# A mixer trunk on one core: another order of the second layer's chunks, and another cost for the first softmax step of a head pair

## The chip, the cores and the metric

The kernel runs on one core of a Trainium2 chip. A core has a matrix engine (TensorE; PE in the profile, its weight loads are PEld), a vector engine (VectorE, DVE), a scalar engine (ScalarE, ACT), GpSimd (POOL) and SyncE (SP), which issues the loads here. Each engine runs its own instructions in the order in which they stand in the program, and waits on semaphores for the others. The metric is the device time of one execution in microseconds (us); lower is better.

## The reference

Two layers work on 256 latent tokens with a prefix of 256 context tokens, width 2048. In each layer one projection of the normalised and modulated input feeds three groups of heads; a gate multiplies each, and one projection leads back:

```python
def _diff_attention(q, k, v, lam):
    ...
        s = jnp.einsum('bqhcd,bkhcd->bhcqk', qq, k).astype(jnp.float32) * scale
        p = jax.nn.softmax(s, axis=-1)
        a = p[:, :, 0] - lam * p[:, :, 1]
        return jnp.einsum('bhqk,bkhe->bqhe', a.astype(v.dtype), v)
```

This is attention with 8 heads, each with two softmaxes that are subtracted. Beside it run a pooling mixer over windows of 2 to 16 tokens, and a convolution module (a gated input, 31 taps, a layer norm, a pointwise product). Shift, scale and gate of each layer (adaLN) come from a vector c by a product with a large matrix, w_mod. Context tokens go through the first layer with the latents and serve the second only as keys and values.

## The kernel before

**Chunks and pieces.** The input projection has 26 chunks of 256 outputs. A chunk's name tells its group: q0 to q3, k0 to k3, v0 to v3 (queries, keys and values of head pairs 0 to 3), u0 and u1 (pool), a0, a1, b0, b1 (convolution), ga0 to ga3 (gates of attention), gp0, gp1 and gc0, gc1 (gates of pool and convolution). `project` computes one as four pieces, each of 24 TensorE products (float32 values are split in a high and a low part, and three of the four products are made). In the first layer there are 512 tokens and a piece has 512 columns (`FULL`); in the second only k and v are for all 512, the other chunks have 256 columns (`HALF`). `ORDER` and `ORDER_1` are the orders of the chunks in the first and the second layer, written by hand; the first layer's loop begins at k0, since b0, a0 and q0 are made while the adaLN sums come in.

**What runs beside the pieces.** After each piece `pump(us)` takes steps from four queues: the context rows of the next layer, `urgent` (attention, pool), `conv_work` and `mod_work`. Each step is a Python generator's, and yields a cost; the pump subtracts it and stops when nothing is left:

```python
    def pump(us):
        for q in (context_work, urgent, conv_work, mod_work):
            while q and us > 0:
                us -= step(q)
```

A pump has 3.4 after a full piece and 0.8 after a half one. `attention` is put in `urgent` when a v chunk is taken, and so runs beside the chunks that follow. `attend_front` makes the scores of one job (`sx`, latent queries; `sc`, context queries, first layer only) and their softmax: the maximum (`mxx`, VectorE, line 634), two exponentials (ScalarE, line 640), reciprocal and scaling (`rx`), and the combination `ex` (ScalarE line 648, VectorE line 649). `attend_back` transposes it on TensorE (`atx`, line 684), splits it in `ahx` (ScalarE) and `alx` (VectorE), and multiplies by the values (`ox`, lines 701 to 703). In names such as `ex0_6_0` the numbers are layer, head and query tile. Taking a q chunk drains `urgent`; taking u1 or v3 drains `conv_work`.

**The adaLN sums.** `mod_on_dve` loads w_mod in tiles of 512 KB (`mraw`, two buffers) and adds each up on VectorE (`macc`, lines 370 and 372), two instructions of it for a tile with two rows, one where only the latents need it. It is the last of the pump's queues. At the end of a unit of 16 tiles TensorE transposes the sums (`modt`). The last two units are put in the queue ahead of the second layer's v1 (`GATES_AT`).

**Order on the engines.** The scheduler of the tile framework places the instructions; each engine then runs them in that order. Weight splits (a cast on ScalarE, line 205, and a subtraction on VectorE, line 206; `in_q_h` and `in_q_l` for a q chunk) and the split of v are given a higher priority and so stand earlier than written. Score tiles and chunk sums share three PSUM buffers, transposes two.

Of the kernel before, what the change touches and what calls it, by code (L numbers as in the profile page):

```python
# [37 lines left out]
    "b0 a0 q0 k0 v0 u0 b1 a1 q1 k1 v1 q2 k2 v2 q3 k3 v3 u1 ga1 gc0 ga2 gp0 ga0 ga3 gp1 gc1"  # L38
).split()
ORDER_1 = (  # L40
    "b0 a0 q0 k0 v0 u0 b1 a1 q1 ga0 k1 v1 q2 k2 gc1 v2 q3 k3 v3 u1 ga1 ga3 gc0 ga2 gp1 gp0"
).split()
OFFSET = {"q": 0, "k": 1024, "v": 2048, "ga": 3072, "u": 4096, "gp": 4608, "a": 5120, "b": 5632, "gc": 6144}

# [7 lines left out]
MOD_TAGS = ("whi", "wlo", "mraw", "whi", "wlo", "mraw", "whi", "wlo")  # L52

FULL, HALF = 3.4, 0.8
FRONT_0 = 2.0
FRONT, BACK = 1.5, 0.7
WAIT_MOD = 4.0
WAIT_CONV = 3.0
# [11 lines left out]
def trunk(  # L70
# [30 lines left out]
    def tmp(name, dt=F32):  # L101
        return tp.tile([P, T], dt, tag="t", name=name)
# [4 lines left out]
    def bank(name):  # L107
        return tr.tile([P, T], F32, tag="tr", name=name)
# [33 lines left out]
    def rsqrt(v, n, name, a=None, y=None):  # L142

        if a is None:
            nc.gpsimd.tensor_tensor(out=v, in0=v, in1=half[:, 0:1].to_broadcast([P, n]), op=ALU.pow)
            return
        nc.vector.tensor_scalar(
            out=y.bitcast(I32), in0=v.bitcast(I32), scalar1=-0.5, scalar2=1597463007.0, op0=ALU.mult, op1=ALU.add
        )
        for step in range(3):  # L150
            nc.vector.tensor_mul(out=a, in0=y, in1=y)
            nc.vector.scalar_tensor_tensor(out=a, in0=a, scalar=-0.5, in1=v, op0=ALU.mult, op1=ALU.mult)
            nc.vector.scalar_tensor_tensor(out=v if step == 2 else y, in0=a, scalar=1.5, in1=y, op0=ALU.add, op1=ALU.mult)
# [469 lines left out]
    def take_v(L, p, ps):  # L623
        L.vh = at.tile([P, 4, WC], F32R, tag="vh", name=f"vh{L.l}_{p}")
        L.vl = at.tile([P, 4, WC], F32R, tag="vl", name=f"vl{L.l}_{p}")
        with tc.high_priority(offset=V_BY):
            split_act(L.vh, L.vl, ps.rearrange("p b (c n) -> p (b c) n", n=WC))
        urgent.append(attention(L, p))
# [33 lines left out]
    def attend_front(L, p, h, which, qt):  # L662

        name = f"{which}{L.l}_{2 * p + h}_{qt}"
        ps = mm.tile([P, 2, T], F32, tag="mm", name=f"s{name}")
        if which == "x":
            scores(L, ps, slice(0, T), h, slice(qt * P, (qt + 1) * P), slice(0, T))
        else:
            for q in range(2):
                scores(L, ps, slice(q * TL, (q + 1) * TL), h, slice(TL + q * P, TL + (q + 1) * P), slice(TL, T))  # L670
        return softmax(L, ps, T, 1, name) if which == "x" else softmax(L, ps, TL, 2, name)

    def attend_back(L, p, h, which, qt, a):
        head = 2 * p + h
        name = f"{which}{L.l}_{head}"
        if qt == 0:
            L.ah = at.tile([P, 4, TL], F32R, tag="ah", name=f"ah{name}")
            L.al = at.tile([P, 4, TL], F32R, tag="al", name=f"al{name}")
        ah, al = L.ah, L.al
        b = bank(f"at{name}_{qt}")  # L680
        if which == "x":
            k0, nk, ts, qs = 0, 4, slice(0, TL), slice(qt * P, (qt + 1) * P)
            for kt in range(4):
                nc.tensor.transpose(b[:, kt * P : (kt + 1) * P], a[:, kt * P : (kt + 1) * P], ident)
            split_act(ah[:, :, qs], al[:, :, qs], b.rearrange("p (k q) -> p k q", q=P))
            if qt == 0:
                return
        else:
            k0, nk, ts = 2, 2, slice(TL, T)
            bv = b.rearrange("p (k q) -> p k q", q=TL)  # L690
            for q in range(2):
                for kt in range(2):
                    nc.tensor.transpose(
                        bv[:, kt, q * P : (q + 1) * P], a[:, q * TL + kt * P : q * TL + (kt + 1) * P], ident
                    )
            split_act(ah[:, :2, :], al[:, :2, :], bv)
        o = bank(f"o{name}")
        hs = slice(h * P, (h + 1) * P)
        for i in range(nk):
            kt = k0 + i  # L700
            nc.tensor.matmul(o[:, :TL], lhsT=L.vh[:, kt, hs], rhs=ah[:, i, :], start=i == 0, stop=False)
            nc.tensor.matmul(o[:, :TL], lhsT=L.vh[:, kt, hs], rhs=al[:, i, :], start=False, stop=False)
            nc.tensor.matmul(o[:, :TL], lhsT=L.vl[:, kt, hs], rhs=ah[:, i, :], start=False, stop=i == nk - 1)
        nc.scalar.copy(out=L.y[head][:, ts], in_=o[:, :TL])
        if which == "x":
            L.osq[h] = tmp(f"osq{name}")
        nc.scalar.activation(L.osq[h][:, ts], o[:, :TL], AF.Square)

    def attention(L, p):
        l, n = L.l, L.n  # L710
        L.osq = [None, None]
        jobs = []
        for h in range(2):
            jobs += [(h, "x", 0), (h, "x", 1)] + ([(h, "c", 0)] if L.ctx else [])
        prev = None
        for j in jobs:
            a = attend_front(L, p, *j)
            yield FRONT if prev else FRONT_0
            if prev:
                attend_back(L, p, *prev)  # L720
                yield BACK
            prev = j + (a,)
        attend_back(L, p, *prev)
        yield BACK

        nh = n // 2
        b = bank(f"ssq{l}_{p}")[:, :nh]
        for h in range(2):
            for half in range(2):
                c = 32 * (2 * h + half)  # L730
                nc.tensor.matmul(
                    b[c : c + 32, :], lhsT=ones[:, 0:32], rhs=L.osq[h][:, half * nh : (half + 1) * nh],
                    start=True, stop=True, skip_group_check=True,
                )
        v = one.tile([P, TL], F32, tag=f"arv{p}", name=f"arv{l}_{p}")[:, :nh]
        nc.vector.tensor_scalar(out=v, in0=b, scalar1=1.0 / P, scalar2=EPS, op0=ALU.mult, op1=ALU.add)
        work = tmp(f"arw{l}_{p}")
        rsqrt(v, nh, f"ars{l}_{p}", work[:, :nh], work[:, TL : TL + nh])
        L.arstd[p] = v
        yield 4.0  # L740
# [488 lines left out]
```

## Time and profile before

| what | value |
|---|---|
| time, median of 3 runs | 1495.96 us (1493.52 to 1496.93) |
| the profiled execution's own time | 1502.84 us |
| its span in the trace | 1501.0 us |
| mean granted clock of TensorE | 0.992 of full speed |
| TensorE busy | 1452.5 us, 97% |
| VectorE busy | 1112.8 us, 74% |
| ScalarE busy | 650.2 us, 43% |
| bytes moved | 258.90 MB, 172 GB/s mean |

The times are of executions without a profile, the rows of one execution with it, whose own time stands in the second line. Starts in rows are us from the begin of its span. A busy share is of the span; the time that an engine stood still ahead of a row is the number in brackets at the row's end, with what ended the waiting behind the arrow.

### The profile page before, as it was taken

The numbers are of one execution on the slowest core, as the hardware profiler recorded it, in microseconds if no ns is written. First come the engines' busy times: TensorE is split into PE (matmuls) and PEld (weight loads), VectorE is DVE, ScalarE is ACT, GpSimd is POOL, SyncE is SP. The second block draws the span as 40 slices with busy tenths as digits, with TensorE's granted clock in tenths as the row PEclk, the third lists the DMA queues.
The fourth block names the chain that finished last, engine by engine and source line by source line (L and its number), as shares of the span: only waits on it lengthen the run. The fifth ranks groups of instructions, "written<-read, shape, count | busy, mean of one in ns | idle before, by whom it ended". The sixth has DMA issues, their size and how long they took to land.

```text
span 1501.0 us, 23277 instructions
## 1 busy us (share of the span) xinstructions
PE 1452.5 (97%) x9196; PEld 1241.8 (83%) x9196; DVE 1112.8 (74%) x1641; ACT 650.2 (43%) x1245; POOL 9.0 (1%) x46
## 2 busy tenths in 40 slices
PE   4999999999999999999999999999999999999997
PEld 3567977897797977888888889988989897999997
DVE  4446999997549865879898964998995567475655
ACT  4224363227546363332433242635545545464543
POOL 0000000000000000000000000000000000000000
PEclk9999999999999999999999999999999999999998
DMA  8995226432234613655667761436733264245553
GB/s 332 397 391 221 81 88 202 148 110 74 74 112 146 202 60 113 221 195 203 209 213 250 243 222 55 142 114 216 265 113 124 79 227 161 99 134 178 187 183 113
DMA packets 75855, 258.90 MB, mean 172 GB/s; under 512 B 8800, under 2 KB 11104, under 8 KB 75744
## 3 DMA queue, kind: packets, MB, share of 16 engines
q1 hardware_dynamic: 75456, 257.14, 49.2%
q8 instruction: 72, 1.18, 0.3%
q14 instruction: 39, 0.32, 0.1%
q10 hardware_dynamic: 288, 0.26, 0.1%
HBM read 255.27 MB, written 2.10 MB: 171 GB/s over the span
## 4 chain that ended last, share of the span: by engine, by line
PE 83%; DVE 7%; DMA 4%; issue 3%; ACT 2%; SPq 0%; POOL 0%; POOLq 0%; DVEq 0%; ACTq 0%
PE ps_o L236 16%; PE ps_k L236 12%; PE ps_ga L236 9%; PE ps_v L227 7%; PE ps_q L236 6%; PE ps_gc L236 5%; PE ps_gp L236 4%; PE ps_first L236 4%; PE ps_b L236 3%; PE ps_u L236 3%; PE ps_a L236 3%; DMA mraw<-in_w_mod 3%; PE modacc L336 2%; DVE s L479 2%; DVE macc L372 1%
## 5 line engine op out<-in xcount | busy, mean ns | idle before, releaser
L372 DVE SCALAR_TENSOR_TENSOR macc<-mraw,c_sb,macc 128x1024 f32<-128x1024 f32 x210 | 262.6, 1280 | 32.2 <-DMA mraw<-in_w_mod 31.5
L236 PE MATMUL ps_o<-yh,out_h 128*128 128x512 f32 (+1 forms) x448 | 151.7, 339 | 0.0
L236 PE MATMUL ps_o<-yl,out_h 128*128 128x512 f32 (+1 forms) x448 | 151.6, 338 | 0.0
L236 PE MATMUL ps_o<-yh,out_l 128*128 128x512 f32 (+1 forms) x448 | 151.6, 338 | 0.0
L227 PE MATMUL ps_v<-in_v_h,hh 128*128 128x256 f32 x512 | 145.2, 284 | 0.0
L227 PE MATMUL ps_v<-in_v_h,hl 128*128 128x256 f32 x512 | 144.8, 283 | 0.0
L227 PE MATMUL ps_v<-in_v_l,hh 128*128 128x256 f32 x512 | 144.3, 282 | 0.0
L479 DVE SCALAR_TENSOR_TENSOR s<-cu,vec,s 128x512 f32<-128x512 f32 (+1 forms) x240 | 136.5, 615 | 0.5
L205 ACT CAST out_h<-out_r 128x1024 fp32r<-128x1024 f32 x56 | 58.8, 1050 | 111.5 <-PE ps_o L236 97.2
L236 PE MATMUL ps_k<-hh,in_k_h 128*128 128x512 f32 x256 | 102.9, 402 | 1.9 <-ACT ex L640 1.0
L236 PE MATMUL ps_k<-hl,in_k_h 128*128 128x512 f32 x256 | 102.1, 399 | 0.0
L236 PE MATMUL ps_k<-hh,in_k_l 128*128 128x512 f32 x256 | 101.8, 398 | 0.0
L227 PEld LDWEIGHTS ps_v<-in_v_l,hh 128*128 128x128 f32 x512 | 96.7, 189 | 0.3
L227 PEld LDWEIGHTS ps_v<-in_v_h,hh 128*128 128x128 f32 x512 | 96.7, 189 | 0.3
L227 PEld LDWEIGHTS ps_v<-in_v_h,hl 128*128 128x128 f32 x512 | 96.4, 188 | 0.0
L236 PEld LDWEIGHTS ps_o<-yl,out_h 128*128 128x128 f32 x448 | 84.3, 188 | 9.9
L236 PEld LDWEIGHTS ps_o<-yh,out_h 128*128 128x128 f32 x448 | 84.3, 188 | 9.9
L236 PEld LDWEIGHTS ps_o<-yh,out_l 128*128 128x128 f32 x448 | 84.3, 188 | 9.8
L206 DVE TENSOR_TENSOR out_l<-out_r,out_h 128x1024 fp32r<-128x1024 f32 x56 | 68.1, 1223 | 32.1 <-ACT out_h L205 30.7
L236 PE MATMUL ps_ga<-hh,in_ga_h 128*128 128x512 f32 (+1 forms) x256 | 87.2, 340 | 1.0 <-ACT ex L640 1.0
L236 PE MATMUL ps_ga<-hl,in_ga_h 128*128 128x512 f32 (+1 forms) x256 | 87.0, 340 | 0.0
L236 PE MATMUL ps_ga<-hh,in_ga_l 128*128 128x512 f32 (+1 forms) x256 | 87.0, 340 | 0.0
(407 smaller groups left out, 3708.2 us busy)
## 6 DMA issues: line engine op xcount, KB each, us to landing
mraw<-in_w_mod SPq DMA_DIRECT2D x128, 512.0 KB, 4.3
wm<-in_w_mod SPq DMA_DIRECT2D x64, 512.0 KB, 8.5
out_r<-in_w_out SPq DMA_DIRECT2D x56, 512.0 KB, 4.0
in_k_r<-in_w_in SPq DMA_DIRECT2D x32, 512.0 KB, 4.4
in_v_r<-in_w_in SPq DMA_DIRECT2D x32, 512.0 KB, 3.4
in_ga_r<-in_w_in SPq DMA_DIRECT2D x32, 512.0 KB, 3.8
in_q_r<-in_w_in SPq DMA_DIRECT2D x28, 512.0 KB, 3.5
in_u_r<-in_w_in SPq DMA_DIRECT2D x16, 512.0 KB, 3.4
```

What stands on the lines that cost most here:

```text
L205: nc.scalar.copy(out=hi, in_=raw)
L206: nc.vector.tensor_sub(out=lo, in0=raw, in1=hi.bitcast(F32))
L227: nc.tensor.matmul(o, lhsT=a[:, ts], rhs=b[:, j, :], start=f and n == 0 and tt % 2 == 0, stop=e and n == 2, skip_group_check=True,)
L236: nc.tensor.matmul(ps[:, nt, t0:t1], lhsT=a[:, j, ns], rhs=b[:, t0:t1], start=f and n == 0, stop=e and n == 2,)
L336: nc.tensor.matmul(acc[c : c + 32, :n], lhsT=sc32[:, k, :], rhs=raw[:, j, :], start=k < 4, stop=k >= KT - 4, skip_group_check=True,)
L372: nc.vector.scalar_tensor_tensor(out=acc[:, r, :], in0=raw, scalar=sc[:, k, r : r + 1], in1=acc[:, r, :], op0=ALU.mult, op1=ALU.add)
L479: nc.vector.scalar_tensor_tensor(out=acc, in0=u[:, :nq, j : j + TL], scalar=w[:, j : j + 1], in1=acc, op0=ALU.mult, op1=ALU.add)
```

## The change

Two things change. `FRONT_0`, the cost that `attention` yields after the first job's scores and softmax, is 2.0 before and becomes one value for each layer, 3.4 and 3.2. In the second layer's order, ga0, gp0 now stand behind v1 and gc1, ga1 behind v2, with no gate chunk between the k and v of a pair, and four gate chunks are left behind u1 where there were six.

```diff
 ORDER_1 = (
-    "b0 a0 q0 k0 v0 u0 b1 a1 q1 ga0 k1 v1 q2 k2 gc1 v2 q3 k3 v3 u1 ga1 ga3 gc0 ga2 gp1 gp0"
+    "b0 a0 q0 k0 v0 u0 b1 a1 q1 k1 v1 ga0 gp0 q2 k2 v2 gc1 ga1 q3 k3 v3 u1 ga2 gc0 ga3 gp1"
 ).split()
...
 FULL, HALF = 3.4, 0.8
-FRONT_0 = 2.0
+FRONT_0 = (3.4, 3.2)
 FRONT, BACK = 1.5, 0.7
...
             a = attend_front(L, p, *j)
-            yield FRONT if prev else FRONT_0
+            yield FRONT if prev else FRONT_0[l]
```

Three places in the order of the engines follow; the first number in a name is the layer, the last is only the program's count.

TensorE in the first layer, pair 0 (chunk u0 runs beside it), from the transpose of the second softmax of head 0 to the first product with the values. Before:

```order
L684 MATMUL atx0_0_1_1922<-ident_82,ex0_0_1_1846 128x128 x4
L236 MATMUL ps_u0_0_1788<-hh0_12_145,in0_u0_3_l_1858 128x512
L236 MATMUL ps_u0_0_1788<-hh0_12_145,in0_u0_3_h_1857 128x512
L236 MATMUL ps_u0_0_1788<-hl0_12_146,in0_u0_3_h_1857 128x512
L236 MATMUL ps_u0_0_1788<-hh0_12_145,in0_u0_3_l_1858 128x512
L701 MATMUL ox0_0_1929<-ahx0_0_1885,vh0_0_1784 128x256
```

After the change:

```order
L684 MATMUL atx0_0_1_1952<-ident_82,ex0_0_1_1876 128x128 x4
L660 MATMUL sx0_1_0_1975<-kh0_0_1528,qh0_0_1362 128x512 x2
L660 MATMUL sx0_1_0_1975<-kl0_0_1529,qh0_0_1362 128x512 x2
L660 MATMUL sx0_1_0_1975<-kh0_0_1528,ql0_0_1363 128x512 x2
L701 MATMUL ox0_0_1959<-ahx0_0_1885,vh0_0_1784 128x256
```

The four products of chunk u0 have moved ahead of the transpose; between it and `ox` stand the next head's scores.

VectorE in the first layer, pair 3 (beside chunk u1), from the last weight split ahead of the pair's softmax to the combination of the first one. Before:

```order
L206 TENSOR_TENSOR in0_u1_1_l_4799<-in0_u1_1_r_4796,in0_u1_1_h_4798 128x1024
L213 TENSOR_TENSOR vl0_3_4792<-ps_v3_0_4550,vh0_3_4791 128x1024
L206 TENSOR_TENSOR in0_u1_3_l_4865<-in0_u1_3_r_4862,in0_u1_3_h_4864 128x1024
L206 TENSOR_TENSOR in0_u1_2_l_4973<-in0_u1_2_r_4970,in0_u1_2_h_4972 128x1024
L634 TENSOR_REDUCE mxx0_6_0_4833<-sx0_6_0_4826 128x2
L634 TENSOR_REDUCE mxx0_6_1_4851<-sx0_6_1_4844 128x2
L644 RECIPROCAL rx0_6_0_4839<-ssx0_6_0_4836 128x2
L645 TENSOR_SCALAR rx0_6_0_4839<-rx0_6_0_4839,neglam0_1345 128x1
L649 SCALAR_TENSOR_TENSOR ex0_6_0_4835<-ex0_6_0_4835,rx0_6_0_4839 128x512
```

After the change:

```order
L213 TENSOR_TENSOR vl0_3_4787<-ps_v3_0_4545,vh0_3_4786 128x1024
L206 TENSOR_TENSOR in0_u1_3_l_4842<-in0_u1_3_r_4839,in0_u1_3_h_4841 128x1024
L372 SCALAR_TENSOR_TENSOR macc0_5_4452<-mraw0_5_11_4783,c_sb_83,macc0_5_4452 128x1024 x2
L634 TENSOR_REDUCE mxx0_6_0_4828<-sx0_6_0_4821 128x2
L206 TENSOR_TENSOR in0_u1_2_l_4927<-in0_u1_2_r_4924,in0_u1_2_h_4926 128x1024
L372 SCALAR_TENSOR_TENSOR macc0_5_4452<-mraw0_5_12_5341,c_sb_83,macc0_5_4452 128x1024
L644 RECIPROCAL rx0_6_0_4834<-ssx0_6_0_4831 128x2
L372 SCALAR_TENSOR_TENSOR macc0_5_4452<-mraw0_5_12_5341,c_sb_83,macc0_5_4452 128x1024
L645 TENSOR_SCALAR rx0_6_0_4834<-rx0_6_0_4834,neglam0_1345 128x1
L372 SCALAR_TENSOR_TENSOR macc0_5_4452<-mraw0_5_13_5397,c_sb_83,macc0_5_4452 128x1024
L649 SCALAR_TENSOR_TENSOR ex0_6_0_4830<-ex0_6_0_4830,rx0_6_0_4834 128x512
```

Five `macc` stand here now (five more follow behind `ex`) where there was none, and a weight split has moved behind the first maximum. The unit of sums before this one, 0_4, is transposed in chunk k3 where it was in q3, and its successors follow it.

VectorE in the second layer, pair 2, from the second maximum of head 4 to the combination of its first softmax. Before:

```order
L634 TENSOR_REDUCE mxx1_4_1_11391<-sx1_4_1_11384 128x2
L372 SCALAR_TENSOR_TENSOR macc1_5_11107<-mraw1_5_10_11295,c_sb_83,macc1_5_11107 128x1024
L644 RECIPROCAL rx1_4_0_11349<-ssx1_4_0_11346 128x2
L206 TENSOR_TENSOR in1_k3_0_l_11462<-in1_k3_0_r_11459,in1_k3_0_h_11461 128x1024
L645 TENSOR_SCALAR rx1_4_0_11349<-rx1_4_0_11349,neglam1_8163 128x1
L644 RECIPROCAL rx1_4_1_11397<-ssx1_4_1_11394 128x2
L634 TENSOR_REDUCE mxx1_5_0_11448<-sx1_5_0_11441 128x2
L649 SCALAR_TENSOR_TENSOR ex1_4_0_11345<-ex1_4_0_11345,rx1_4_0_11349 128x512
```

After the change:

```order
L634 TENSOR_REDUCE mxx1_4_1_11388<-sx1_4_1_11381 128x2
L206 TENSOR_TENSOR in1_ga1_0_l_11459<-in1_ga1_0_r_11456,in1_ga1_0_h_11458 128x1024
L644 RECIPROCAL rx1_4_0_11346<-ssx1_4_0_11343 128x2
L372 SCALAR_TENSOR_TENSOR macc1_5_11107<-mraw1_5_10_11295,c_sb_83,macc1_5_11107 128x1024
L645 TENSOR_SCALAR rx1_4_0_11346<-rx1_4_0_11346,neglam1_8163 128x1
L644 RECIPROCAL rx1_4_1_11394<-ssx1_4_1_11391 128x2
L634 TENSOR_REDUCE mxx1_5_0_11445<-sx1_5_0_11438 128x2
L649 SCALAR_TENSOR_TENSOR ex1_4_0_11342<-ex1_4_0_11342,rx1_4_0_11346 128x512
```

The same instructions stand here, but the weight split (of ga1 now, of k3 before) has moved ahead of the `macc`.

## Rows read from the trace of the kernel before

**Rows 1.** The page, part 1: busy us, share of the span, instructions.
```profile
PE 1452.5 (97%) x9196; PEld 1241.8 (83%) x9196; DVE 1112.8 (74%) x1641; ACT 650.2 (43%) x1245; POOL 9.0 (1%) x46
```

**Rows 2.** TensorE's waits: us in total, times, longest.
```profile
PE atx L684 <- DVE ex L649: 8.5, 5, 3.6
```

**Rows 3.** Timeline of TensorE, layer 0: start, length, instruction, idle before it.
```profile
185.12 0.40 PE L236 MATMUL ps_u<-hh,in_u_h 128*128 128x512 f32 x1
...
190.48 0.40 PE L236 MATMUL ps_u<-hh,in_u_l 128*128 128x512 f32 x1
...
199.45 0.66 PE L684 MATMUL atx<-ident,ex 128*128 128x128 f32 x4 [0.53 <-DVE ex L649]
...
200.37 0.40 PE L660 MATMUL sx<-kh,qh 64*128 64x512 f32 x2
200.60 0.40 PE L660 MATMUL sx<-kl,qh 64*128 64x512 f32 x2
...
211.31 0.39 PE L701 MATMUL oc<-ahc,vh 128*128 128x256 f32 x1 [0.55 <-ACT ahc L212]
...
385.50 1.16 PE L160 MATMUL cln_rstd<-ident,cln_v 128*128 128x128 f32 x8 [0.88 <-POOL cln_v L145]
...
455.33 0.66 PE L684 MATMUL atx<-ident,ex 128*128 128x128 f32 x4 [1.55 <-DVE ex L649]
...
539.61 0.36 PE L701 MATMUL ox<-ahx,vh 128*128 128x256 f32 x1 [0.65 <-DVE alx L213]
```

**Rows 4.** The same of layer 1.
```profile
1034.69 0.66 PE L684 MATMUL atx<-ident,ex 128*128 128x128 f32 x4 [2.56 <-DVE ex L649]
...
1165.72 0.50 PE L236 MATMUL ps_k<-hh,in_k_h 128*128 128x512 f32 x1 [1.03 <-ACT ex L640]
...
1246.36 0.66 PE L684 MATMUL atx<-ident,ex 128*128 128x128 f32 x4 [3.61 <-DVE ex L649]
```

**Rows 5.** Windows: us, busy (instructions) of each engine, granted clock, DMA share, GB/s.
```profile
1035.50:1038.90 3.40, 3.40 (x18) 3.40 (x17) 3.40 (x7) 2.08 (x6) 0.00 (x0) 0.50 0.59 189
...
1247.10:1253.90 6.80, 6.80 (x21) 4.47 (x20) 6.03 (x10) 5.47 (x12) 0.00 (x0) 0.50 0.53 191
1253.90:1260.70 6.80, 6.80 (x38) 5.79 (x38) 5.73 (x8) 2.74 (x5) 0.00 (x0) 1.00 0.69 219
```

**Rows 6.** Instructions by shape: count, shortest/mean/longest ns, first to last start.
```profile
L205 ACT CAST in_k_h<-in_k_r x32: 1029/1048/1057, 126.7 to 1259.7; 128x1024 fp32r<-128x1024 f32 x32
L212 ACT CAST ahx<-atx x32: 562/586/605, 200.1 to 1327.0; 128x512 fp32r<-128x512 f32 x32
L213 DVE TENSOR_TENSOR alx<-atx,ahx x32: 668/683/697, 201.9 to 1328.2; 128x512 fp32r<-128x512 f32 x32
L751 ACT ACTIVATE sga<-ps_ga x16: 374/484/599, 588.5 to 1375.7; 128x512 f32<-128x512 f32 x8, 128x256 f32<-128x256 f32 x8
```

**Rows 7.** Timeline of VectorE, layer 1, pair 2.
```profile
1239.18 1.22 DVE L634 TENSOR_REDUCE mxx<-sx 128x2 f32<-128x1024 f32 x1
1241.85 1.28 DVE L372 SCALAR_TENSOR_TENSOR macc<-mraw,c_sb,macc 128x1024 f32<-128x1024 f32 x1 [1.45 <-DMA mraw<-in_w_mod]
...
1243.13 1.20 DVE L206 TENSOR_TENSOR in_k_l<-in_k_r,in_k_h 128x1024 fp32r<-128x1024 f32 x1
...
1245.57 0.74 DVE L649 SCALAR_TENSOR_TENSOR ex<-ex,rx 128x512 f32<-128x512 f32 x1
```

**Rows 8.** Timeline of VectorE, layer 0, pair 2 (first row) and pair 3.
```profile
449.49 2.48 DVE L372 SCALAR_TENSOR_TENSOR macc<-mraw,c_sb,macc 128x1024 f32<-128x1024 f32 x2
...
524.53 1.23 DVE L213 TENSOR_TENSOR vl<-ps_v,vh 128x1024 fp32r<-128x1024 f32 x1 [3.19 <-ACT vh L212]
...
529.91 1.23 DVE L206 TENSOR_TENSOR in_u_l<-in_u_r,in_u_h 128x1024 fp32r<-128x1024 f32 x1 [3.02 <-ACT in_u_h L205]
```

**Rows 9.** Timeline of ScalarE, layer 1, pair 2.
```profile
1236.21 1.28 ACT L640 ACT_TABLE_LOAD   x1
1237.51 0.69 ACT L640 ACTIVATE ex<-sx,mxx 128x512 f32<-128x512 f32 x1
```

## The prediction

> **What bounds the kernel now.** I read first the page's busy shares [rows 1]: TensorE works 97% of the span, every other engine well under that. So the time can only change where TensorE stands still or runs at its lower clock. Next the list of waits [rows 2]: inside the two layers the largest entry is the transpose of a finished softmax (`atx`, line 684), which waits for VectorE's combination of the two softmaxes (`ex`, line 649) five times, 8.5 us in all. Then I followed TensorE's own rows through each of the eight pairs. In the first layer the waits are small: 0.53 us before the first transpose of pair 0, 0.55 before a context product, 0.88 in the convolution's norm beside pair 1, 1.55 before the first transpose of pair 2, 0.65 before the attention product of pair 3 [rows 3]. In the second layer two waits stand out, 2.56 us in pair 0 and 3.61 in pair 2, and two of 1.03 us (one is shown), where a new chunk waits for a PSUM buffer that the softmax still reads [rows 4]. Behind each of the two long ones the granted clock is 0.50, the 1.2 GHz level: for 3.4 us after the one and 6.8 after the other, in which TensorE ran 21 rows, against 38 in the 6.8 us that follow [rows 5]. After the waits of 1.55 and 1.03 no stretch at 0.50 follows. All that this change touches is therefore about 18 us: some 5 of waits in the first layer, 8 of waits and 5 of lost clock (half of 10.2 us) in the second.
>
> **The change, part by part.** First what it doesn't do. A pump's budget is local: a step's cost is taken from the pump in which it runs and no debt is carried on. In the second layer an attention always begins in a pump of 0.8 or less, and any step of 0.8 or more ends it; 2.0 and 3.2 give the same program. The "four pieces" of the second layer cost and bring nothing. What is left is 3.4 in the first layer, and the second layer's order.
>
> *First layer, 3.4.* The first softmax now gets a pump to itself, and a whole piece of 24 products stands behind its scores. A piece takes 5.6 us: 23 steps between its first row at 185.12 and its last at 190.48, 0.233 each [rows 3]. What comes after it is packed closer: the second transpose is no longer followed by products of the chunk but by the next scores alone, and the attention product stands right behind those.
>
> Pair 0 (chunk u0). Before, the waits sum to 0.53 + 0.20 (a second transpose, part of the 8.5) + 0.55 = 1.3 us. The cover between the second transpose and the product `ox` was four products and is now three score rows, 0.23 from one to the next [rows 3]. That product needs `ahx` (0.59 on ScalarE) and then `alx` (0.68 on VectorE) [rows 6], and on ScalarE a weight cast of 1.05 [rows 6] now stands ahead of `ahx`. If the cast starts as the transpose ends, `ox` waits 1.05 + 0.59 - 0.7 = 0.95 us; if it is over by then, 0. The nearest row is the 0.65 of pair 3, where `ox` already waits for `alx` behind a short cover [rows 3], so it is likely no zero; I take 0.95, 0.35 for the row that needs `alx`, and 1.7 for the rest, namely 0.7 for the first transpose (a little over its 0.53) and 0.25, 0.4 and 0.35 where context and second head follow. Sum 3.0, so **+1.7** (bounds -0.5 and +3).
>
> Pair 1: the same packing, +0.5; but the convolution's norm has fewer products as cover and its VectorE step one place earlier, so that 0.88 falls to about 0.4: **0** (bounds -0.9 and +1).
>
> Pair 2 (chunk q3): the transposes of the adaLN sums move half a chunk on, and the multiply-accumulates (`macc`, 1.28 us each [rows 7]) that stood between this pair's maxima and its `ex` stand there no more. Its 1.55 goes; the packing brings 0.7: **-0.8** (bounds -1.5 and +0.3).
>
> Pair 3 (chunk u1) gets them instead. Before, VectorE had nothing to do there: 3.19 and 3.02 us of idle stood just ahead of the softmax [rows 8]. Now ten `macc` stand from `vl` on, two of them ahead of the first maximum and three, with a weight split, between it and `ex`. Chain: 1.2 for the maximum, 1.2 for the split (weight splits and maxima are 1.20 to 1.22 long), 3 x 1.2, 0.75 for `ex`: 6.8 us. Cover: the piece's 5.6 and 1.0 of scores. That alone is 0.2; the two `macc` ahead of the maximum and a late load add to it. Above it is bounded by the 3.61 of the second layer [rows 4], where a load was late. It is nearest to pair 2's 1.55, where four `macc` stood between maximum and `ex` (the row at 449.49 holds the first two [rows 8]). I take 1.2, and 1.4 for the `ox` and `alx` waits behind it, against 0.65 before: **+1.9** (bounds 0 and +5).
>
> First layer: 1.7 + 0 - 0.8 + 1.9 = **+2.8**.
>
> *Second layer.* Pair 0 has the same neighbours in both orders: 2.56 and its 3.4 us at half clock stay. Pair 1 now runs beside ga0 and gp0 and not beside q2 and k2. On ScalarE a table load and two gates stand ahead of the last `ahx`, 1.28 + 2 x 0.48 = 2.2 us [rows 6, 9], on VectorE their products; half of it lies under TensorE's half pieces, with half the columns and so about 2.8 us each: **+1.0** (bounds 0 and +2.2). Pair 2 now runs beside gc1 and ga1. Before, VectorE idled 1.45 us for a load ahead of a `macc` at 1241.85, and ran a weight split of 1.20 after it, at 1243.13; `ex` began at 1245.57 [rows 7]. Now the split stands ahead of that `macc`, in the idle time, so `ex` starts 1.2 us earlier: -1.2, if the split's weights are cast by 1240.4 (they are one chunk's first, loaded as early as those before). A wait of 2.4 lies near the 2.56 of pair 0, and I give it that one's 3.4 us at half clock in place of 6.8: -1.7 (bounds 0 and -3.4). A table load and two gates ahead of this pair's last `ahx` too: +0.3 (0 to +1). Pair 2: **-2.6**. Pair 3 and the gate chunks behind it move, but the waits of 1.03 come from a PSUM buffer and stay: 0. Second layer: **-1.6**.
>
> **The sum** is +2.8 - 1.6 = +1.2 us on the profiled execution's 1502.84. That is 6.9 us above the median of the runs shown, 1495.96; on this median it gives **1497.1 us**. A measurement of this kernel tells a change from none at about 0.2%, 3.0 us; the forecast is no measurable change.
>
> **A rule against the trace.** The change adds two table loads, 18 to 20. The row shows 1.28 us for one at 1236.21, and the next `Exp` begins at 1237.51, 0.02 us after its end [rows 9]; I count 1.28. The Trainium skill ("ScalarE: Activation LUTs", section What ACT_TABLE_LOAD costs) gives 1283 ns for the load, with which the trace agrees, and about 1380 ns of drain more at every switch, which this row does not show. By that the two would cost, as an estimate, up to 2.8 us more, and the sum would be +4.0.
>
> **Rivals.**
> 1. *The cover works* (faster). The packing costs nothing, since `ahx` finds ScalarE free: the first layer's `atx` waits go (0.53, 0.20 and 1.55) and nothing comes in their place: -2.3. In pair 2 of the second layer the wait gets so short that the clock stays at 1.00: -1.2 - 3.4. Pair 1 costs 0.6. In all -6.3: about 1490. For it: no half clock after 1.55. Against it: 2.4 lies nearer to 2.56, and 0.65 in pair 3 shows that `ox` waits under a short cover. The two parts need not come together; the larger alone, with the other's waits only halved, gives about 1493. Chance 0.18.
> 2. *The `macc` in pair 3* (slower). TensorE waits there for `ex0_6_0` 3.0 us and not 1.2, because one of the `macc` ahead of it waits for its load as at 1241.85 (+1.8), and the clock falls to 0.50 for 3.4 us behind it (+1.7): +4.7, **1500.6**. It decides from a wait as long as the 2.56 of the second layer's pair 0, that is with one late load of 1.45 on top of my 1.2. For it: ten `macc` in a stretch that had 6.2 us of idle. Against: the loads have two buffers and are issued well before. Chance 0.22.
> 3. *The change does nothing on the path.* As 3.2 is dead, 3.4 and the gates may only move idle time from one transpose to the next: 0, 1496. Chance 0.15.
> 4. *The added table loads lie whole on the path* in pairs 1 and 2, 2 x 1.28, of which about 0.8 is counted: +1.8 more, **1499**. Against it: ScalarE is busy 43% and waits for TensorE before most of its work. [...] Chance 0.08.
>
> **How the numbers follow.** My forecast, +1.2 with its terms off by a microsecond or two, has 0.37. Below -3.0 us lies nearly all of rival 1 and a little of the forecast: faster 0.19. Above +3.0 lie rival 2, part of rival 4 and of the forecast: slower 0.27. Same: 0.54. The range reaches to 1492.5, the half of rival 1, and to 1501.5, just past rival 2.
>
> **What would show it.** In the profile after: in pair 0 an `ox` row with about 1 us of idle before it, released by `ahx`; in pair 2 of the first layer no `atx` wait over 0.3; in pair 3 an `atx` wait of about 1.2; in pair 2 of the second layer one of about 2.4 with 3 to 4 us at 0.50 behind it; the 2.56 of pair 0 unchanged. I am wrong if the sum of waits in the first layer does not rise, if the clock falls somewhere in the first layer, or if pair 2's wait is still above 3 us or below 1.6.

## The result, and the profile after

The changed kernel takes 1504.06 us (median of 5 runs, 1502.72 to 1508.43), the one before 1495.96 (5 runs, 1493.52 to 1498.2). The ratio is 1.006, interval 1.0039 to 1.0081: about 8 us slower, outside the range that I gave, and on the other side of "no measurable change". The two profiled executions don't show it: their spans are 1501.3 and 1501.0 us. That is the first thing to explain, and its cause is one of the mistakes in the prediction.

The page of the changed kernel has TensorE's busy time of [rows 1] to the digit, and the other engines' within 2.3 us; so the difference is to be looked for in waits and clock again.

```profile
PE 1452.5 (97%) x9196; PEld 1241.1 (83%) x9196; DVE 1111.9 (74%) x1641; ACT 652.5 (43%) x1247; POOL 8.8 (1%) x46
```

TensorE's waits after the change (us in total, times, longest), beside [rows 2]: the transposes of `ex` wait less in all, 7.8 for 8.5, and the two largest new entries are `modt` behind ScalarE and `ox` behind `ahx`.

```profile
PE atx L684 <- DVE ex L649: 7.8, 5, 2.3
...
PE modt L383 <- ACT modj L387: 2.7, 1, 2.7
...
PE ox L701 <- ACT ahx L212: 1.9, 4, 0.6
```

TensorE's rows with idle time, first layer and then second, against [rows 3, 4]:

```profile
197.09 0.66 PE L684 MATMUL atx<-ident,ex 128*128 128x128 f32 x4 [0.55 <-DVE ex L649]
...
205.71 0.38 PE L701 MATMUL ox<-ahx,vh 128*128 128x256 f32 x1 [0.17 <-ACT ahx L212]
...
384.10 1.16 PE L160 MATMUL cln_rstd<-ident,cln_v 128*128 128x128 f32 x8 [0.31 <-POOL cln_v L145]
...
457.62 0.39 PE L701 MATMUL ox<-ahx,vh 128*128 128x256 f32 x1 [0.49 <-ACT ahx L212]
...
536.46 0.66 PE L684 MATMUL atx<-ident,ex 128*128 128x128 f32 x4 [2.32 <-DVE ex L649]
...
893.77 1.12 PE L383 MATMUL modt<-ident,macc 128*128 128x128 f32 x4 [2.72 <-ACT modj L387]
...
1039.18 0.66 PE L684 MATMUL atx<-ident,ex 128*128 128x128 f32 x4 [2.30 <-DVE ex L649]
...
1160.77 0.66 PE L684 MATMUL atx<-ident,ex 128*128 128x128 f32 x4 [0.24 <-DVE s L761]
...
1249.69 0.66 PE L684 MATMUL atx<-ident,ex 128*128 128x128 f32 x4 [2.20 <-DVE ex L649]
```

The 1.55 of pair 2 is gone, pair 3 has 2.32 in its place, and a wait of 2.72 stands at 893.77, in the output projection, far from any softmax. Behind both the clock falls. The windows of this kernel behind the waits of 2.32, 2.72 and 2.20 (columns as in [rows 5]) show 0.75 and 0.74, 0.58, and 1.00:

```profile
536.40:539.80 3.40, 3.34 (x19) 2.69 (x20) 3.40 (x6) 2.35 (x6) 0.00 (x0) 0.75 0.28 87
539.80:543.20 3.40, 3.40 (x12) 2.67 (x12) 3.40 (x5) 2.23 (x9) 0.00 (x0) 0.74 0.52 169
893.70:897.10 3.40, 3.33 (x13) 2.94 (x14) 1.99 (x4) 2.66 (x21) 0.00 (x0) 0.58 0.84 302
1249.70:1253.10 3.40, 3.38 (x21) 2.36 (x22) 3.40 (x5) 2.71 (x6) 0.00 (x0) 1.00 0.72 263
```

**Why pair 3 waits.** VectorE's rows there, from the macc ahead of the maximum to `ex`:

```profile
527.23 2.48 DVE L372 SCALAR_TENSOR_TENSOR macc<-mraw,c_sb,macc 128x1024 f32<-128x1024 f32 x2
529.62 1.22 DVE L634 TENSOR_REDUCE mxx<-sx 128x2 f32<-128x1024 f32 x1
530.76 1.22 DVE L206 TENSOR_TENSOR in_u_l<-in_u_r,in_u_h 128x1024 fp32r<-128x1024 f32 x1
531.89 1.28 DVE L372 SCALAR_TENSOR_TENSOR macc<-mraw,c_sb,macc 128x1024 f32<-128x1024 f32 x1
...
535.66 0.74 DVE L649 SCALAR_TENSOR_TENSOR ex<-ex,rx 128x512 f32<-128x512 f32 x1
```

No row waits for a load. The chain from the maximum to the end of `ex` is 6.8 us (529.62 to 536.40), as worked out; that it starts late, behind two macc of 2.4 us, is what I had undersized. The last of the scores that the maximum needs is TensorE's row

```profile
526.96 0.40 PE L660 MATMUL sx<-kh,ql 64*128 64x512 f32 x2
```

which ends at 527.36; the maximum begins 2.3 us later, and 2.32 is the wait.

**Why 893.77 waits.** The transposes of the last unit of sums (`modt`) now stand between chunks o5 and o6, where they stood in the middle of o5. There are two PSUM buffers for them, and the third group needs ScalarE's copies (`modj`) of the first. ScalarE's rows:

```profile
890.68 1.05 ACT L205 CAST last_0qh<-last_r 128x1024 fp32r<-128x1024 f32 x1 [6.38 <-DMA last_r<-in_w_out]
891.63 1.04 ACT L205 CAST out_h<-out_r 128x1024 fp32r<-128x1024 f32 x1
892.58 0.27 ACT L387 ACTIVATE modj<-modt 128x128 f32<-128x128 f32 x1
```

and SyncE's just before, where the load of that weight is issued behind one of `mraw`:

```profile
884.95 0.33 SPq L356 DMA_DIRECT2D mraw<-in_w_mod  x1
886.08 1.46 SPq L189 DMA_DIRECT2D last_r<-in_w_out  x2
```

ScalarE idles 6.38 us for `last_r`, casts two weights, and only then copies. In the order of before, the copies stand ahead of that cast, and no load of `mraw` stands close ahead of that of `last_r`. ScalarE's rows and SyncE's of the kernel before:

```profile
878.01 0.27 ACT L387 ACTIVATE modj<-modt 128x128 f32<-128x128 f32 x1
...
882.91 1.05 ACT L205 CAST last_0qh<-last_r 128x1024 fp32r<-128x1024 f32 x1 [0.68 <-DMA last_r<-in_w_out]
```

```profile
879.39 7.92 SPq L189 DMA_DIRECT2D last_r<-in_w_out  x3
```

There the load is issued at 879.39, 6.7 us earlier than after the change, and the cast waits 0.68 us for it.

### The profile page after: what moved, and what is told of

The parts are those of the page before. It is cut to its first block, busy times and chain, and to the rows that moved or that the text cites. A ratio compares the mean times of both kernels' runs of the same rounds, so it can differ in the third digit from the quotient of the medians.

```text
span 1501.3 us, 23262 instructions
## 1 busy us (share of the span) xinstructions
PE 1452.5 (97%) x9196; PEld 1241.1 (83%) x9196; DVE 1111.9 (74%) x1641; ACT 652.5 (43%) x1247; POOL 8.8 (1%) x46
## 4 chain that ended last, share of the span: by engine, by line
PE 78%; DVE 10%; DMA 5%; issue 3%; ACT 3%; SPq 0%; POOL 0%; POOLq 0%; DVEq 0%; ACTq 0%
PE ps_o L236 15%; PE ps_k L236 11%; PE ps_ga L236 9%; PE ps_q L236 7%; PE ps_v L227 5%; PE ps_gp L236 5%; PE ps_first L236 4%; PE ps_gc L236 4%; PE ps_b L236 3%; PE ps_a L236 3%; DMA mraw<-in_w_mod 2%; DVE macc L372 2%; PE ps_u L236 2%; DVE s L479 2%; PE modacc L336 2%
```

## The experiments

Fifteen kernels ran, in four sets, each set on one chip with runs of the kernel before among them; ratios are to those. I use two measures: the times, and in the trace the length of a stretch from the first row of one chunk to the first of a later one.

**Second trace, and the two halves.** The first set held the kernel before itself, and each half of the change:

```diff
-FRONT_0 = 2.0
+FRONT_0 = (3.4, 2.0)          # e2, with the old ORDER_1
...
-... q1 ga0 k1 v1 q2 k2 gc1 v2 q3 ...   # e3, with FRONT_0 = 2.0
+... q1 k1 v1 ga0 gp0 q2 k2 v2 gc1 ga1 q3 ...
```

> The kernel before, unchanged: a second trace of it, since its median (1495.96) and its profiled execution (1502.84) are 6.9 us apart. If the 6.9 us are one stretch of that one execution, this trace shows a shorter stretch somewhere and the rest alike, time 1494 to 1498. If the traces of one kernel differ everywhere by this much, no stretch stands out and single traces tell little.

> The first layer's 3.4 alone, with the second layer's old order. Theory A (the loss is the first layer's: the softmax of pair 3 waits behind the macc, and the transposes of the last sums stand at the boundary of o5 and o6 behind a cast that waits for a load): 1502 to 1508, that is +6 to +12, with the atx wait of about 2.3 in pair 3 and the modt wait in the output projection. Theory B (the second layer's gates cost more than their trace shows): 1496, no change.

> The second layer's new order alone, 2.0 kept. Theory A: the second layer takes 4.4 us less, as between the traces of before and after: 1490 to 1493. Theory B: 1500 or more.

Measured: 1496.39 for the control (ratio 0.9995, 0.9982 to 1.0008); 1501.37 for the first layer's half (1.0026, 1.0011 to 1.0041), with the `atx` wait of 2.77 in pair 3 and the `modt` wait of 2.61; 1499.02 for the order (1.0009, 0.9998 to 1.0019). So theory A has both waits of the first layer right, with a time a little under its range (1502 to 1508), and misses for the second: the new order does not give 4.4 us. The control's trace says why. Its span is 1493.5, and its TensorE rows in the second layer's pairs 0 and 2 are

```profile
1033.47 0.66 PE L684 MATMUL atx<-ident,ex 128*128 128x128 f32 x4 [1.73 <-DVE ex L649]
...
1241.93 0.66 PE L684 MATMUL atx<-ident,ex 128*128 128x128 f32 x4 [2.23 <-DVE ex L649]
```

where the first trace had 2.56 and 3.61 [rows 4]. On VectorE, the macc that idled 1.45 us for its load [rows 7] does not idle here, and the clock behind pair 2 stays at 1.00:

```profile
1237.43 1.28 DVE L372 SCALAR_TENSOR_TENSOR macc<-mraw,c_sb,macc 128x1024 f32<-128x1024 f32 x1
...
1241.13 0.74 DVE L649 SCALAR_TENSOR_TENSOR ex<-ex,rx 128x512 f32<-128x512 f32 x1
```

```profile
1241.90:1245.30 3.40, 3.35 (x19) 2.29 (x20) 3.40 (x5) 2.68 (x6) 0.00 (x0) 1.00 0.75 257
1245.30:1248.70 3.40, 3.40 (x20) 2.87 (x19) 3.40 (x7) 2.75 (x7) 0.00 (x0) 1.00 0.69 231
```

That late load and the 6.8 us at half clock belonged to the one execution that I read. So did something in pair 0: of the 7.5 us between the two spans, 4.6 lie from the second layer's b1 to its first output chunk o0 (356.8 against 352.2), and 2.4 in chunk u0 ahead of it (21.4 against 19.0), where the wait of 2.56 had 3.4 us of half clock behind it and the control's 1.73 has none. Over six traces with the old order and its macc in place (the first, e1, e2, e6, e11, e15), the wait of pair 2 is 3.61, 2.23, 2.02, 1.86, 1.96, 1.86, and only the first has half clock behind it.

**The boundary by itself, taken away and made.** In e4 the changed kernel's later sums come back to the middle of chunks; in e6 the kernel before gets them at the boundaries, with softmax and orders untouched.

```diff
-            pump(FULL if toks[1] - toks[0] == T else HALF)
+            pump(FULL + (0.7 if name == 'ga1_0' or name == 'gc0_0' and n < 2 else 0.0) if ...   # e4
+            pump(FULL - (1.1 if name == 'ga1_0' or name == 'gc0_0' and n < 2 else 0.0) if ...   # e6
```

> The whole change, and in the first layer six pumps of chunks ga1 and gc0 get 0.7 more, so that the transposes of the sums from unit 0_5 on stand in the middle of chunks again as before the change, the last unit's in the middle of o5. Theory A: the modt wait of 2.7 us and the half clock behind it in the output projection go: 4 to 5 us less than after, about 1499.5. Rival C: the load (last_r) is late for its own reasons and TensorE waits for it a little later: 1504, as after.

> The kernel before, softmax steps and both orders untouched; only six pumps of the first layer's chunks ga1 and gc0 get 1.1 less, so that the sums from unit 0_5 on are transposed half a chunk later, the last unit's at the boundary of o5 and o6. Theory A (the boundary costs by itself, since ScalarE's copies of the sums stand behind a cast that waits for last_r): the modt wait of 2.6 us with the half clock behind it, +4 to +5: about 1501. Rival C (the late load comes from what the softmax change moved, not from the boundary): no wait there, 1497.

Measured: e4 1500.64 (1.0025, 1.0014 to 1.0035), without the `modt` wait, and 0.0020 to 0.0035 under the changed kernel's ratios in the other sets (3.0 to 5.2 us); e6 1500.8 (1.0025, 1.0011 to 1.004), with it:

```profile
541.58 0.35 PE L701 MATMUL ox<-ahx,vh 128*128 128x256 f32 x1 [0.65 <-DVE alx L213]
...
895.34 1.11 PE L383 MATMUL modt<-ident,macc 128*128 128x128 f32 x4 [2.95 <-ACT modj L387]
```

A wait and 3.6 us more (1500.8 - 1497.21, the kernel before in that set) come from the place of the later units' sums alone; rival C falls. The late `last_r` comes with that place: it is issued at 887.38 in e6 and ScalarE idles 6.61 us for it, at 880.12 in e4 with 0.61 us.

**The changed kernel again, and pair 3.** e7 puts 0.7 more into the pumps of v2 and k3, so that the sums are done before pair 3 and back at their old places afterwards.

```diff
+            pump(FULL + (0.7 if name in ('v2_0', 'k3_0') else 0.0) if toks[1] - toks[0] == T else HALF)
```

> The changed kernel itself, a second time: a second trace of it, and its time beside the kernels of this set. By the stages of the traces so far (first layer +7 of which 4 to 5 stand at the boundary of o5 and o6, second layer +1.6): 1503 to 1506, and the modt wait of 2.6 to 2.7 us in the output projection stands in this trace too. If that wait was a chance of two traces: about 1500, as with the sums back in the middle of chunks.

> The whole change, and the pumps of chunks v2 and k3 in the first layer get 0.7 more: unit 0_5 is summed up before pair 3 begins, and no macc stands among the softmax steps of pair 3; they stand beside pair 2 again, and the last unit is transposed in the middle of o5. Theory A (pair 3's wait is the macc's): no atx wait over 0.5 in pair 3, no modt wait; 6 to 7 us less than the changed kernel, about 1498. Rival (pair 3 waits because the second transpose and its product are packed closer): the 2.3 to 2.8 us in pair 3 stay, about 1500.

Measured: e5 1503.54 (1.0049, 1.0035 to 1.0064); its `modt` wait is 1.88 and the `atx` wait of pair 3 2.55. e7 1501.4 (1.0032, 1.002 to 1.0045). Its rows of TensorE with idle time in pairs 2 and 3 are only these two; neither the wait of pair 3 nor that of `modt` is there:

```profile
453.32 0.66 PE L684 MATMUL atx<-ident,ex 128*128 128x128 f32 x4 [1.07 <-DVE ex L649]
...
544.32 0.38 PE L701 MATMUL ox<-ahx,vh 128*128 128x256 f32 x1 [0.73 <-ACT ahx L212]
```

So pair 3's wait was the macc's. But the time fell by 2 us, not 6 to 7. The trace of e5 and that of e7 both have, in the second layer, what the first trace of the changed kernel lacked: half clock behind pair 2, after a wait of 2.22 and 2.24. The windows of e5:

```profile
1249.40:1252.80 3.40, 3.40 (x17) 2.26 (x17) 3.40 (x5) 2.73 (x6) 0.00 (x0) 0.75 0.70 242
1252.80:1256.20 3.40, 3.40 (x15) 3.14 (x15) 3.34 (x7) 2.68 (x7) 0.00 (x0) 0.50 0.68 207
```

**Is it the macc in the second layer's pair 2?** e8 starts the last two units earlier; e9 and e10 leave seven macc out, in the old and the new order.

```diff
-GATES_AT = "v1"
+GATES_AT = "v0"                                              # e8
...
-                else:
+                elif (l, u) != (1, 5) or not 7 <= k < 14:    # e9, e10
```

> The kernel before, but the last two units of adaLN sums of the second layer are put in the queue ahead of v0 instead of v1: no macc is left beside the second layer's pair 2, and one more stands between maxima and ex of pair 0. Theory D (pair 2's wait of 2.0 to 3.6 us is the macc's and its load's, in either order of the chunks): that wait falls under 0.6 and its half clock goes, -2.5 to -3.5, pair 0 gets up to +1.2: about 1494.5. If pair 2's wait has another cause: it stays near 2, and the time at 1497 or above.

> The kernel before, old order, with seven macc instructions of the second layer's unit 1_5 (tiles 7 to 13) left out, their loads kept: part of the adaLN sum of one gate is missing. Theory D (the second layer's pair 2 waits for ex because of macc and their loads, and how late a load is differs from one execution to the next): no atx wait over 0.6 in pair 2, no stretch at 0.50 there, 2 to 3 us less than before in the median, about 1494.5. If the wait has another cause, it stays near 2.

> The second layer's new order alone, with the same seven macc left out. Theory D: pair 2's wait goes here too, and what is left of the new order is pair 1 and pair 3, 0.9 + 0.5: the time stands 1 to 2 us above the same omission in the old order, about 1496. Theory E (the gates cost beside pair 2 also without macc, by table loads and gates ahead of its last ahx): 3 us or more above it, with waits of ox or of a chunk in pair 2.

Measured: 1502.08 for e8 (1.0033, 1.0019 to 1.0048), 1497.61 for e9 (1.0005, 0.9993 to 1.0017), 1498.32 for e10 (1.0011, 1.0 to 1.0022). In all three the wait ahead of pair 2's first transpose is gone, so its cause was the macc, by their own length or their waiting for loads, which these runs don't part; in none is the time gained. In e8 VectorE's splits of two weights come late instead:

```profile
1203.30 0.39 PE L236 MATMUL ps_gc<-hh,in_gc_l 128*128 128x256 f32 x1 [1.10 <-DVE in_gc_l L206]
...
1208.01 0.52 PE L227 MATMUL ps_v<-in_v_l,hh 128*128 128x256 f32 x1 [1.84 <-DVE in_v_l L206]
```

In e9 the next macc that is left waits for its load, and `alx` stands behind it: TensorE's row, and VectorE's.

```profile
1248.45 0.39 PE L702 MATMUL ox<-alx,vh 128*128 128x256 f32 x1 [1.71 <-DVE alx L213]
```

```profile
1245.31 1.28 DVE L372 SCALAR_TENSOR_TENSOR macc<-mraw,c_sb,macc 128x1024 f32<-128x1024 f32 x1 [2.68 <-DMA mraw<-in_w_mod]
```

In e10 that macc idles 3.16 us for its load, and the second head's transposes wait 2.49 us. Theory D is right on the cause and wrong on the worth; as the omission moved the wait, e9 and e10 say little on the order's price.

**The packing alone, and four corners on one chip.** What the two halves cost together did not yet add up (1.0009 for the order, 1.0032 for e7). e11 is e7 with the old order; e12 to e15 are the changed kernel, e3, e7 and e11 again, in one set.

> The first layer's 3.4 with the old order of the second, and the pumps of v2 and k3 with 0.7 more, so that neither pair 3 nor the boundary of o5 and o6 has the sums: what is left is the packing of each pair's softmax and product. By the traces so far (pair 0 -0.5, pair 1 +0.4, pair 2 +0.2, pair 3 +0.1): no change, 1496 to 1498. If the packing costs what I forecast for pairs 0 and 3 (1.7 and 1.9): 1500.

> The changed kernel once more, as the first corner of one set on one chip: old or new order of the second layer, with the first layer's sums late (as the change has them) or early. If the parts add up: 1503 to 1505.

> The new order alone, again. Theory F (the order costs little, 1 to 2 us: pair 1 and pair 3): 1497 to 1499, ratio near 1.001. Theory G (the order costs 4 to 6 us, and the first measurement of it was low): ratio 1.003 or more.

> The whole change with the first layer's sums early, again: neither pair 3 nor the boundary waits. Theory F: the order's 1 to 2 us are all that is left, ratio near 1.001, and the 1.0032 of its first set was that set's. Theory G: 1.003 again, with a stretch at half clock beside the second layer's pair 2.

> The same with the old order of the second layer, again: between 0.998 and 1.000 by its first measurement. The difference to the run before this one is the order's price by itself: 1 to 2 us by theory F, 4 to 6 by theory G.

| kernel | median us | ratio, interval |
|---|---|---|
| e11: 3.4, sums early, old order | 1495.94 | 0.9992, 0.9982 to 1.0002 |
| e15: the same, in the last set | 1496.63 | 0.9995, 0.9981 to 1.001 |
| e13: new order alone | 1498.6 | 1.0005, 0.9993 to 1.0018 |
| e14: 3.4, sums early, new order | 1500.02 | 1.0015, 1.0004 to 1.0027 |
| e12: the changed kernel | 1505.06 | 1.0045, 1.003 to 1.0061 |

3.4 without its effect on the sums costs nothing that can be measured. The moved sums cost 5.0 us in this set (e12 less e14; 2.1 in the set of e5 and e7), the order 1.5 (e13 less the 1497.12 of before in this set) to 3.4 us (e14 less e15). The times are nearer to theory F, though e13's interval and e3's include no change at all; theory G's sign, the half clock beside pair 2, stands in the traces of both e13 and e14. No version beat the kernel before measurably; e11 and e15 come closest.

The traces give the order more: from the second layer's b1 to its o0, five of the six old-order traces named above (all but the first) took 351.4 to 352.2 us, and eight of the new order (after, e3, e4, e5, e7, e12, e13, e14) 353.8 to 357.8. Two of the eight (after, e4) have no half clock behind pair 2 and took 353.8 and 353.9; the six others took 356.2 to 357.8. So in these traces the order costs about 2 us, and 2 to 4 more where the clock falls. The first trace, from which I forecast, took 356.8.

## Why the prediction was wrong

**Second layer, pair 2 (-2.6 forecast).** This is the step that failed first. Of the kernel after I had the wait right, about 2.4 (1.85 to 2.99 in eight traces), but not the 3.4 us at half clock that I put behind it for 6.8 before: five traces have 6.8 us there, one 3.4 and two none. One of the five is e12,

```profile
1253.30:1260.10 6.80, 6.80 (x28) 5.22 (x27) 6.14 (x10) 5.34 (x12) 0.00 (x0) 0.50 0.58 189
```

so the term of -1.7 has no support. And what I subtracted from was not the kernel before, but one execution of it in which a load came late. I had noted that this execution's time lay 6.9 us above the median and carried the difference along as a constant; a part of it sat in the very rows that I booked as gain (356.8 against 351.4 to 352.2). With the usual 1.9 to 2.2 us and no half clock as the start, the forecast wait and clock are a loss there, not a gain. That is also why the two first traces have equal spans.

**Where the sums go (a term left out).** In pair 2 I wrote that "the transposes of the adaLN sums move half a chunk on", and priced only what that freed. Every later unit moves too, and the last one falls on the boundary where its copies stand behind ScalarE's wait for `last_r`. That is 3.6 us by time (e6). From chunk o0 to the last chunk the three traces of the changed kernel took 165.6, 164.1 and 167.4 us against 160.5, of which about 1 us is moved there from the gate chunks (193.1 for 194.1).

**First layer, pair 3 (+1.9 forecast).** The mechanism was right, the term mis-sized: waits of 2.32, 2.55 and 2.07 where I took 1.2, and behind each the clock down, which I had left to rival 2. Chunk u1 took 37.7, 39.1 and 38.8 us for 34.7: +3.0 to +4.4 in those traces. In e4, the same program up to there, the wait is 2.51 and the clock stays at 1.00; u1 took 36.3, +1.6. So the wait without the fall costs about what I forecast, since `ox` waits 0.6 behind it where I took 1.4 for `ox` and `alx`, and the rest goes with the fall. A fall of the clock in the first layer was one of my signs of being wrong. What came is rival 2 in place and kind, without the late load that I asked for; the two macc ahead of the maximum were enough for the wait.

**Pair 0 (+1.7) and pair 1 (0).** The packing costs nothing: chunk u0 took 34.5 us for 34.9, and `ox` waits 0.17, not 0.95. The weight cast ahead of `ahx` starts while the transposes of 204.05 still run, and not after them:

```profile
204.05 0.60 PE L684 MATMUL atx<-ident,ex 128*128 128x128 f32 x4
...
204.14 1.03 ACT L205 CAST in_b_h<-in_b_r 128x1024 fp32r<-128x1024 f32 x1
205.08 0.57 ACT L212 CAST ahx<-atx 128x512 fp32r<-128x512 f32 x1
```

Pair 1's norm wait fell to 0.31, as forecast, and its `ox` took 0.60. e11 and e15 confirm the sum of it.

**Pair 2 of the first layer (-0.8).** The 1.55 went, `ox` waits 0.49. The transposes of unit 0_4 stood at the end of chunk v2 and in q3 and stand in k3 now: v2 took 22.8 for 23.8, q3 34.0 for 35.9, k3 28.9 for 26.7. In all -0.7, as good as forecast.

**Second layer, the rest.** 2.0 and 3.2 did give one program: e3 and the changed kernel run the same rows in the same order there. Pair 0 is as forecast in the first trace (2.30 for 2.56), but the 2.56 was one execution's too: over the sixteen traces other than e8's this wait runs from 1.45 to 2.94, with half clock behind it in ten, in either order. Pair 1 waits 0.24 more besides the 1.03 that moved to gp0, where I took 1.0. The added table loads took their 1.28 and no drain: the changed kernel's row at pair 2, with the step ahead of it and the gate behind,

```profile
1257.84 0.73 ACT L648 ACTIVATE ex<-ex,rx 128x512 f32<-128x512 f32 x1
1258.59 1.28 ACT L768 ACT_TABLE_LOAD   x1
1259.88 0.66 ACT L768 ACTIVATE sg<-ps_gc 128x256 f32<-128x256 f32 x2
```

stand 0.01 to 0.02 us apart, as in [rows 9]. Here, too, the 1380 ns of drain that the Trainium skill gives ("ScalarE: Activation LUTs", What ACT_TABLE_LOAD costs) does not show, on either side of the load. No TensorE row waits behind this load, so rival 4 has no row for it.

**What stays open.** By its three traces the changed kernel loses 8 to 15 us against the control (6.7 to 9.5 from the first layer's k0 to its last chunk, 1.6 to 5.5 from b1 to o0 of the second), by time 6.3 to 8.1. Part of that is which execution the trace shows: those of e5 and e12 took 1505.88 and 1508.66, 2.3 and 3.6 above their medians, the control's 1495.24, 1.2 below its own. A trace is one execution; how often the kernel before has a late load or half clock in an execution that leaves no trace isn't known, and I did not settle it. The price of the order, 1.5 to 3.4 us, is not known better than that, and why the clock falls behind pair 2 in six of eight traces of the new order and in none of the five usual ones of the old isn't shown. Nor is it shown where the 2 us without a fall lie: e4's stretch from b1 to o0 is 1.7 us longer than the control's (353.9 against 352.2), and TensorE stands still for 4.8 us of it in both.

## What to carry to other kernels

When the profiled execution is slower than the median, ask which rows hold the excess before booking any row as gain; a wait for a load in one trace is the first suspect, and a second trace of the same kernel costs less than the mistake. When a step gets a larger share of a budget, follow all work that is last in that queue to its end, and read at each new place what stands ahead of it on the engines that it needs: here the dearest effect of a softmax knob stood over 300 us behind the last softmax that it touched.

## What the runs showed of the hardware

Waits of TensorE of nearly one length had different clocks behind them: 2.23 us in the control and 2.20 in the changed kernel were followed by 1.00, 2.22 in e5 by 0.75 and then 0.50. In the first layer's pair 3, 2.32 in the changed kernel was followed by 0.75 and 0.74, and 2.51 in e4 by 1.00:

```profile
538.50:541.90 3.40, 3.34 (x22) 2.70 (x23) 3.40 (x6) 2.35 (x6) 0.00 (x0) 1.00 0.17 67
541.90:545.30 3.40, 3.40 (x16) 2.78 (x15) 3.40 (x5) 2.23 (x9) 0.00 (x0) 1.00 0.26 71
```

In the second layer's pair 0, waits of 1.65 in e7 and of 1.65 in e15 were followed by a fall in the one (first row) and by none in the other:

```profile
1032.60:1036.00 3.40, 3.35 (x20) 3.36 (x21) 3.40 (x6) 2.94 (x7) 0.00 (x0) 0.67 0.61 192
...
1032.90:1036.30 3.40, 3.38 (x27) 3.24 (x27) 3.40 (x6) 3.10 (x8) 0.00 (x0) 1.00 0.49 160
```

From these rows the length of the wait alone doesn't tell whether the clock falls; what does, the runs don't show.
